# Convolution taps of a two-layer decoder trunk: none beside layer A's output products, more beside layer B's input products

## The chip, the cores and the metric

The kernel runs on one core of a Trainium2 chip, as one program. The metric is the device time of an execution in microseconds. Three runs of the kernel before give a median of 1700.62 us (1698.21 to 1704.68). Five engines work side by side, each through its own queue in order: TensorE (PE, matrix products and transposes), VectorE (DVE), ScalarE (ACT), GpSimd (POOL) and SyncE (SP, which issues transfers).

## What is computed

Two layers on x, 2048 rows of 1024 columns in float32. Each layer l first makes u = x * (1 + scale) + shift, with shift, scale and gate from the vector c. The mixer of layer A is

```
[a | g | z] = u W_in + b_in;  h = a * sigmoid(g)
h = causal depthwise conv_31(h) + b_conv;  h = LayerNorm_channels(h);  h = swish(h)
y = (h * silu(z)) W_out + b_out
```

and that of layer B

```
[B | C | v | z] = u W_in;  y = (B * conv_3(C * v) * silu(z)) W_out
```

and both end in x <- LayerNorm(alpha * x + gate * y). The convolution with 31 taps is per channel, along the rows.

## The kernel before

**Products.** The rows are cut into two halves (sc 0 and 1), and each half into two quarters of 512 rows, so that quarters q = 0 to 3 exist. An input product W_in for a half is done with seven products of half the size in place of eight (a Strassen form, class Pair: the seven parts of a pair of weight blocks). Each of the seven is 12 matmuls of 512 columns (four blocks, each operand split into a high and a low part). A list fixes their order (order_of). TensorE's instructions are kept in the order of the program; the instructions of the other engines are ordered by a planner at build time, which takes the ready instruction that stands earliest in the program, with instructions inside `urgent()` ahead of the rest.

**Stages.** Layer A's input products for half 0, then for half 1 (12 pairs each, tiles pxa, pya, pza and pxz, pyz, pzz); layer A's output products for quarters 0 and 1 (tile po); layer B's input products for half 0 (16 pairs, 112 products; tiles pxc, pyc, pzc, pxb, pyb, pzb); layer A's output products for quarters 2 and 3; layer B's input products for half 1; layer B's output products for the four quarters. The input of layer B is made in the output blocks: evacuate (L842, L843, L846, L848), the power on GpSimd (L849), finish (L809, L812), the transposes of columns (tile ptx) and L834, and then the sums and splits of u_stages (join; L279 and L225 on tiles ub). For layer B's first half the weights are made in the stage (L355, L357 on VectorE, splits L224 on ScalarE and L225 on GpSimd) and stored; for its second half they are loaded as stored.

**The long convolution.** It runs on VectorE, one tap an instruction (L572, mac). For each of the 8 blocks of 128 channels and each half of the rows conv_a puts 47 steps into the queue todo: begin (a load of h on SP's queue, preparations on ScalarE and GpSimd), 27 taps of the even and odd positions into two PSUM banks (pca, pcb), turn, out_even (L604, the first result), both_less (L610), 15 taps of the sum of both (pca, pcd), and out_odd (L625, the second result). A result is a tile of tag acc, of which there are three (BUFS), and the convolution's banks are two (BANKS, conv). given stores a result on SP's queue and defers statistics by LAG = 8 ticks: four transposes on TensorE (tile pl) and four bn_stats on VectorE (L668), after which the result's buffer is free. While a norm is being made, statistics wait (held).

**What sets how many steps are issued.** Behind each product or output group stands a call of tick, which takes as many steps from todo as its rate says, carries the fraction on, and then runs what has been deferred to this tick:

```
        due_taps[0] += taps
        conv_steps(int(due_taps[0]))
        due_taps[0] -= int(due_taps[0])
```

The rates are in RATE: a = 3.2 a product in layer A, b = 3.4 a product in layer B's first half, o = 1 for each of the 16 groups of a quarter's output products (run_out). From the sixth part of the last pair but one on (the place `(a, 6)` in ending) the norm of the quarter runs beside the last 9 products, and there the rate is 1. Ahead of it need(q) issues four steps at a time, with no product between, until the quarter's statistics are all there. A planner's order isn't the order of issue: VectorE may do a step before or after the product behind which it is issued.

The same code runs ending for layer A's second half (q = 0) and for layer B's first half (q = 2), and run_out for quarters 0 and 1 with taps still in todo, and for quarters 2 and 3 with todo empty.

Of the kernel before, what the change touches and what calls it, by code (L numbers as in the profile page):

```python
# [30 lines left out]
BOOST = 100000  # L31
BUFS = dict(u=56, raw=4, s=1, w=5, ta=8, hin=1, xk=2, xs=1, pt=1, acc=3, tv=2, uf=6)
BANKS = dict(mm=4, tp=2, conv=2)
RATE = dict(a=3.2, b=3.4, o=1)
LAG = 8
LEAD = 3

# [2 lines left out]
def hybrid_trunk(ctx, tc, x, c, ada_w, ada_b, a_w_in, a_b_in, a_conv_w, a_conv_b,  # L40
# [42 lines left out]
    def flush(after=None):  # L83
        with ExitStack() as order:
            if after is not None:
                order.enter_context(tc.issue_after(after.ins))
            for dst, src, _ in late:
                nc.scalar.dma_start(dst, src)
        for *_, then in late:
            if then is not None:  # L90
                then()
        late.clear()
# [24 lines left out]
    def tick(taps, *gens):  # L117
        clock[0] += 1
# [3 lines that stand above are left out]
        for gen in gens:  # L122
            next(gen, None)
        due = [job for at, job in waiting if at <= clock[0]]
        waiting[:] = [w for w in waiting if w[0] > clock[0]]
        for job in due:
            job()
# [299 lines left out]
    def product(pair, p, ks=range(KH)):  # L427
        for i in ks:
            pair.mm(p, i)
            if i == KH - 1:  # L430
                pair.evacuate(p)
# [238 lines left out]
    def conv_steps(n):  # L670
        for _ in range(min(n, len(todo))):
            todo.popleft()()
# [106 lines left out]
    def out_rows(q, l):  # L779
        wide = lambda ap: (lambda h: ap[:, h * T:(h + 1) * T].broadcast_to([P, T]))  # L780
        rows = [row_tiles(f"g{l}_{q}", wide(post_ln_g[l:l + 1, :])),
                row_tiles(f"b{l}_{q}", wide(post_ln_b[l:l + 1, :]))]
        if l == 0:
            rows.append(row_tiles(f"gb{q}", lambda h: gb_dram[h]))
        return rows
# [183 lines left out]
    def queue_convs():  # L969

        while wanted and all(wanted[0] + (hf,) in windows for hf in range(2)):
            conv_a(*wanted.popleft())
# [103 lines left out]
    for n, (p, r) in enumerate(order_a):  # L1076
# [9 lines left out]
        queue_convs()  # L1086
        tick(1 if (p, r) in moves else RATE["a"])
    flush()
# [3 lines left out]
    norms = {q: a_norm(q, gs[0, q]) for q in range(NQ)}  # L1092
# [3 lines left out]
    def begin_out(q, l, rows):  # L1096
        if l == 0:
            fu[q] = [st("u", [P, T], f"ub{q}_{k}") for k in range(K)]
        outs[l, q] = mixer_out(q, l, gs[l, q], rows, fu.get(q))
        next(outs[l, q])  # L1100
# [7 lines left out]
    def run_out(l, q, *beside):  # L1108
        for _ in outs[l, q]:
            tick(RATE["o"], *beside)  # L1110
        for gen in beside:
# [12 lines left out]
    def need(q):  # L1124

        while emitted[q] < K:
            tick(4)

    def ending(pairs, order, rate, q, *beside):

        a, b = len(pairs) - 2, len(pairs) - 1
        gens = list(beside)
        for p, r in order:
            if (p, r) == (b, 5):
                rows = out_rows(q, 0)
            if (p, r) == (a, 6):
                need(q)
                gens.append(norms[q])
            product(pairs[p], r)
            queue_convs()  # L1140
            tick(1 if norms[q] in gens else rate, *gens)
        for gen in gens:
            for _ in gen:
                pass
        flush()
        begin_out(q, 0, rows)
        return rows

    rows = ending(pa[1], order_a, RATE["a"], 0, back)
    need(1)  # L1150
    run_out(0, 0, wait(6, norms[1]))
# [12 lines left out]
    def with_join(sc, order):  # L1164
        for n, at in enumerate(order):
            if n == 6:
                join(sc)
            yield at

    for pair in pb[0]:  # L1170
        pair.adds = (nc.vector, nc.gpsimd)
    rows = ending(pb[0], with_join(0, order_b), RATE["b"], 2)
    need(3)
    run_out(0, 2, wait(6, norms[3]))
# [46 lines left out]
```

## Time and profile before

| | |
|---|---|
| median of three runs | 1700.62 us |
| the profiled execution's own time | 1698.88 us |
| its span, first to last instruction | 1696.8 us |
| mean granted clock of TensorE | 0.963 |
| busy: TensorE, VectorE, ScalarE, GpSimd | 92%, 69%, 39%, 57% |

The span is 2.1 us shorter than the execution's own time. The rows further down are of this one execution. A row of the timeline gives the start, the duration, engine, line, operation, output and input, a count, and in brackets the idle time ahead of it and what ended it. In a table by stretch each engine has its busy time and its instructions, and then come TensorE's granted clock (1.00 is full speed), the share of the transfer engines and their rate. Stages by their first matmul: layer A's output products of quarter 0 at 588.5 us, layer B's first input product at 696.9; in the second half the same places are at 1077.3 and 1179.2.

### The profile page before, as it was taken

The numbers are of one execution on the slowest core, as the hardware profiler recorded it, in microseconds if no ns is written. First come the engines' busy times: TensorE is split into PE (matmuls) and PEld (weight loads), VectorE is DVE, ScalarE is ACT, GpSimd is POOL, SyncE is SP. The second block draws the span as 40 slices with busy tenths as digits, with TensorE's granted clock in tenths as the row PEclk, the third lists the DMA queues.
The fourth block names the chain that finished last, engine by engine and source line by source line (L and its number), as shares of the span: only waits on it lengthen the run. The fifth ranks groups of instructions, "written<-read, shape, count | busy, mean of one in ns | idle before, by whom it ended". The sixth has DMA issues, their size and how long they took to land.

```text
span 1696.8 us, 20882 instructions
## 1 busy us (share of the span) xinstructions
PE 1568.5 (92%) x6828; PEld 1267.6 (75%) x6828; DVE 1171.5 (69%) x1820; ACT 665.7 (39%) x1134; POOL 963.8 (57%) x808
## 2 busy tenths in 40 slices
PE   5899998799998998869998998999899999999996
PEld 5777787678887777647777886777688888778884
DVE  6669999978988988888999953574822222225565
ACT  3544445655433436543444334254632221212221
POOL 5788878775654245866888786537655531221110
PEclk9799999899999999979999999999899999999999
DMA  9478888799999997526777767976689886778995
GB/s 271 157 275 294 293 302 302 243 350 363 330 371 352 359 329 242 196 96 240 270 241 254 268 247 270 385 255 236 221 281 301 297 302 215 247 268 267 336 333 209
DMA packets 237916, 469.63 MB, mean 277 GB/s; under 512 B 20329, under 2 KB 102641, under 8 KB 237809
## 3 DMA queue, kind: packets, MB, share of 16 engines
q1 hardware_dynamic: 190864, 323.06, 56.8%
q10 hardware_dynamic: 46944, 145.25, 22.1%
q8 instruction: 54, 0.88, 0.2%
q14 instruction: 54, 0.43, 0.1%
HBM read 297.72 MB, written 170.52 MB: 276 GB/s over the span
## 4 chain that ended last, share of the span: by engine, by line
PE 52%; DVE 21%; DMA 12%; POOL 7%; issue 5%; ACT 2%; ACTq 0%; SPq 0%; DVEq 0%; POOLq 0%
PE po L98 19%; PE pxb L98 6%; PE pxc L98 6%; DVE pca L572 5%; PE pxa L98 4%; DVE pcb L572 4%; PE pzb L98 3%; DMA keptb<-wb 3%; PE pzc L98 3%; DMA keptc<-wc 2%; PE pza L98 2%; PE pxz L98 2%; DMA wr<-w_dram 2%; PE pyc L98 1%; DVE pcd L572 1%
## 5 line engine op out<-in xcount | busy, mean ns | idle before, releaser
L572 DVE SCALAR_TENSOR_TENSOR pcb<-h,w,pcb 128x512 f32<-128x512 f32 x224 | 166.5, 743 | 9.0 <-ACT pcb L580 8.6
L572 DVE SCALAR_TENSOR_TENSOR pca<-h,w,pca 128x512 f32<-128x512 f32 x192 | 142.7, 743 | 0.2
L572 DVE SCALAR_TENSOR_TENSOR pca<-xs,w,pca 128x512 f32<-128x512 f32 x128 | 95.4, 745 | 0.8
L842 DVE TENSOR_TENSOR r<-po,r 128x512 f32<-128x512 f32 x64 | 43.2, 681 | 68.1 <-PE po L98 49.5
L572 DVE SCALAR_TENSOR_TENSOR pcd<-xs,w,pcd 128x512 f32<-128x512 f32 x112 | 83.2, 743 | 0.1
L517 POOL TENSOR_TENSOR ada<-ada,adaw 128x512 f32<-128x512 f32 x48 | 63.6, 1325 | 34.4 <-ACT adaw L511 14.3
L812 ACT ACTIVATE r<-r,nb,rs 128x512 f32<-128x512 f32 x64 | 47.2, 809 | 81.3 <-DVE nb L809 81.2
L225 POOL TENSOR_TENSOR gb_0l<-vb,gb_0h 128x512 fp32r<-128x512 f32 x4 | 5.2, 1292 | 111.2 <-ACT gb_0h L224 111.2
L547 POOL TENSOR_TENSOR wf<-wf,grow 128x512 f32<-128x512 f32 x32 | 42.4, 1331 | 38.2 <-DMA wf<-in_b_w_out_dram 33.4
L849 POOL TENSOR_TENSOR rs<-rs,mhalf 128x1 f32<-128x1 f32 x32 | 18.3, 584 | 75.5 <-DVE rs L848 75.5
L586 POOL TENSOR_TENSOR lead<-lead,part 128x512 f32<-128x512 f32 x32 | 43.6, 1361 | 22.0 <-ACT part L585 22.0
L911 POOL TENSOR_TENSOR hb1c<-c12c,c22c 128x512 f32<-128x512 f32 x16 | 21.1, 1322 | 59.6 <-DVE c22c L403 59.6
L225 POOL TENSOR_TENSOR wc<-rawc,wc 128x512 fp32r<-128x512 f32 x32 | 45.1, 1409 | 16.8 <-ACT wc L224 16.7
L511 ACT ACTIVATE adaw<-adaw,cond 128x512 f32<-128x512 f32 x64 | 42.4, 715 | 30.4 <-DMA adaw<-in_ada_w_dram 27.4
L225 POOL TENSOR_TENSOR wf<-wf 128x512 fp32r<-128x512 f32 x32 | 42.9, 1350 | 17.6 <-ACT wf L224 17.6
L821 DVE TENSOR_TENSOR r<-r,g 128x512 f32<-128x512 f32 x48 | 39.0, 825 | 20.1 <-PE ptx L101 17.7
L803 POOL TENSOR_TENSOR r<-r,gb 128x512 f32<-128x512 f32 x32 | 44.8, 1416 | 13.3 <-DMA r<-in_x_dram 11.5
L834 ACT ACTIVATE ub<-ptx,post_sh,post_sc 128x128 f32<-128x128 f32 x128 | 47.2, 487 | 12.9 <-PE ptx L101 12.9
L225 POOL TENSOR_TENSOR wb<-sb,wb 128x512 fp32r<-128x512 f32 x24 | 35.3, 1473 | 23.7 <-ACT wb L224 23.7
L225 POOL TENSOR_TENSOR wb<-rawb,wb 128x512 fp32r<-128x512 f32 x32 | 44.7, 1398 | 6.3 <-ACT wb L224 4.0
L225 POOL TENSOR_TENSOR wa<-rawa,wa 128x512 fp32r<-128x512 f32 x32 | 44.9, 1407 | 4.0 <-ACT wa L224 2.4
L756 ACT ACTIVATE v<-v,second_columns 128x512 f32<-128x512 f32 x32 | 25.9, 814 | 51.0 <-DVE v L755 50.8
(1388 smaller groups left out, 5582.9 us busy)
## 6 DMA issues: line engine op xcount, KB each, us to landing
wr<-w_dram SPq DMA_DIRECT2D x128, 512.0 KB
kepta<-wa ACTq DMA_DIRECT2D x56, 512.0 KB
wa<-kepta SPq DMA_DIRECT2D x56, 512.0 KB
keptc<-wc ACTq DMA_DIRECT2D x56, 512.0 KB
keptb<-wb ACTq DMA_DIRECT2D x56, 512.0 KB
wc<-keptc SPq DMA_DIRECT2D x56, 512.0 KB
wb<-keptb SPq DMA_DIRECT2D x56, 512.0 KB
adaw<-in_ada_w_dram SPq DMA_DIRECT2D x32, 512.0 KB
```

The costliest lines, as they stand in the source:

```text
L98: return tc.keep_in_program_order(nc.tensor.matmul(*args, **kw))
L225: made = (eng or nc.gpsimd).tensor_tensor(lo, src, hi.bitcast(F32), op=ALU.subtract)
L511: nc.scalar.activation(raw[:, j], raw[:, j], AF.Identity, scale=cond[:, kk + j:kk + j + 1])
L517: nc.gpsimd.tensor_tensor(acc, acc, raw[:, j], op=ALU.add)
L547: nc.gpsimd.tensor_tensor(w[:, 1], w[:, 1], grow, op=ALU.mult)
L572: nc.vector.scalar_tensor_tensor(out=tiles[out], in0=src, scalar=w, in1=tiles[acc], op0=ALU.mult, op1=op)
L586: nc.gpsimd.tensor_tensor(lead, lead, part, op=ALU.add)
L803: nc.gpsimd.tensor_tensor(rt, rt, gb[0][h], op=ALU.add)
L812: nc.scalar.activation(rts[t, h], rts[t, h], AF.Identity, scale=rs, bias=nb)
L821: eng.tensor_tensor(r, r, g[h], op=ALU.mult)
L834: nc.scalar.activation(fs[k][:, t * P:(t + 1) * P], pt[:, j * P:(j + 1) * P], AF.Identity, scale=post_sc[:, k:k + 1], bias=post_sh[:, k:k ...
L842: nc.vector.tensor_tensor(r, pss[t], r, op=ALU.add)
```

## The change

Two rates and the number of steps beside a norm. In ending and run_out no steps are issued beside a norm and beside layer A's output products; behind each of layer B's input products of the first half 3.8 steps are issued instead of 3.4. (RATE's o serves layer B's output products as well, where todo is empty.)

```diff
--- before.py
+++ after.py
@@ -31,7 +31,7 @@
 BOOST = 100000
 BUFS = dict(u=56, raw=4, s=1, w=5, ta=8, hin=1, xk=2, xs=1, pt=1, acc=3, tv=2, uf=6)
 BANKS = dict(mm=4, tp=2, conv=2)
-RATE = dict(a=3.2, b=3.4, o=1)
+RATE = dict(a=3.2, b=3.8, o=0)
 LAG = 8
 LEAD = 3
 
@@ -1138,7 +1138,7 @@
                 gens.append(norms[q])
             product(pairs[p], r)
             queue_convs()
-            tick(1 if norms[q] in gens else rate, *gens)
+            tick(0 if norms[q] in gens else rate, *gens)
         for gen in gens:
             for _ in gen:
                 pass
```

## Rows read from the trace of the kernel before

**Rows 1.** The page: busy times of the engines, shares of the last chain.

```profile
PE 1568.5 (92%) x6828; PEld 1267.6 (75%) x6828; DVE 1171.5 (69%) x1820; ACT 665.7 (39%) x1134; POOL 963.8 (57%) x808
PE 52%; DVE 21%; DMA 12%; POOL 7%; issue 5%; ACT 2%; ACTq 0%; SPq 0%; DVEq 0%; POOLq 0%
```

**Rows 2.** Busy time by stretch: PE, PEld, DVE, ACT, POOL; clock, transfer share, GB/s.

```profile
651.00:697.00 46.00, 41.37 (x187) 32.47 (x185) 39.58 (x60) 20.36 (x48) 34.85 (x28) 0.93 0.79 254
697.00:766.30 69.30, 48.97 (x178) 35.53 (x177) 59.59 (x83) 38.82 (x80) 46.88 (x36) 0.78 0.32 119
777.00:971.60 194.60, 184.01 (x799) 147.63 (x798) 185.67 (x288) 78.20 (x132) 153.61 (x135) 0.98 0.70 249
766.30:1005.60 239.30, 228.62 (x998) 183.81 (x997) 213.84 (x334) 96.33 (x163) 188.56 (x165) 0.99 0.70 252
980.00:1041.00 61.00, 58.56 (x258) 47.23 (x258) 25.53 (x45) 20.05 (x34) 44.15 (x39) 1.00 0.72 255
...
1136.20:1179.20 43.00, 39.19 (x178) 31.07 (x177) 20.87 (x31) 18.68 (x44) 33.29 (x27) 0.96 0.65 214
1179.20:1227.10 47.90, 42.69 (x178) 32.72 (x177) 38.94 (x55) 32.73 (x69) 31.16 (x17) 0.89 0.70 238
```

**Rows 3.** By stretch, the taps (L572) alone: VectorE's busy time, clock, transfers.

```profile
614.30:660.20 45.90, 0.00 (x0) 0.96 0.74 255
660.30:714.00 53.70, 29.42 (x42) 0.87 0.63 202
714.00:777.00 63.00, 0.00 (x0) 0.81 0.44 163
777.00:971.60 194.60, 119.94 (x168) 0.98 0.70 249
```

**Rows 4.** Timeline of VectorE at two second results of convolutions.

```profile
658.91 0.88 DVE L668 BATCH_NORM_STATS2 s<-pl 128x6 f32<-128x128 f32 x4
659.71 0.67 DVE L625 TENSOR_TENSOR acc<-pca,acc 128x512 f32<-128x512 f32 x1
...
773.45 0.88 DVE L668 BATCH_NORM_STATS2 s<-pl 128x6 f32<-128x128 f32 x4
774.25 0.67 DVE L625 TENSOR_TENSOR acc<-pca,acc 128x512 f32<-128x512 f32 x1
```

**Rows 5.** Groups of the page: GpSimd's additions in begin.

```profile
L586 POOL TENSOR_TENSOR lead<-lead,part 128x512 f32<-128x512 f32 x32 | 43.6, 1361 | 22.0 <-ACT part L585 22.0
```

**Rows 6.** Groups by line, 777 to 971.6, VectorE: the convolutions' results.

```profile
L604 DVE SCALAR_TENSOR_TENSOR acc<-pca,second_columns,pt 128x512 f32<-128x512 f32 x4 | 3.0, 745 | 2.1 <-ACT pt L599 2.1
L625 DVE TENSOR_TENSOR acc<-pca,acc 128x512 f32<-128x512 f32 x4 | 2.7, 686 | 0.2
```

**Rows 7.** Timelines at layer B's start, first half, then second half.

```profile
697.03 0.74 DVE L572 SCALAR_TENSOR_TENSOR pcd<-xs,w,pcd 128x512 f32<-128x512 f32 x1
697.68 0.68 DVE L842 TENSOR_TENSOR r<-po,r 128x512 f32<-128x512 f32 x1
...
703.94 1.97 PE L101 MATMUL ptx<-ident,r 128*128 128x128 f32 x8 [4.17 <-ACT r L812]
...
706.13 0.63 PE L98 MATMUL pyc<-ub00b21l,wc 128*128 128x512 f32 x1
706.56 0.63 PE L98 MATMUL pyc<-ub00b21h,wc 128*128 128x512 f32 x1
...
724.35 5.12 DVE L279 TENSOR_TENSOR ub<-ub,ub 128x512 f32<-128x512 f32 x3
...
1183.00 0.39 PE L98 MATMUL pyc<-ub10b21l,wc 128*128 128x512 f32 x1
1183.23 0.40 PE L98 MATMUL pyc<-ub10b21h,wc 128*128 128x512 f32 x1
...
1198.58 3.09 DVE L279 TENSOR_TENSOR ub<-ub,ub 128x512 f32<-128x512 f32 x5
```

**Rows 8.** TensorE's waits on VectorE, 766.3 to 1005.6: total, times, longest.

```profile
PE pxb L98 <- DVE c22b L403: 2.3, 1, 2.3
```

## Prediction

> **What bounds the kernel now.** I read the page's busy shares first: TensorE is busy 92% of the span, VectorE 69%, and in the chain that ended last TensorE has 52% and VectorE 21% [rows 1]. So TensorE sets the time, and VectorE where it makes TensorE wait. The table by stretch shows where that is [rows 2]. Layer A's second output block of the first half (651 to 697) takes 46.0 us, its twin in the second half (1136.2 to 1179.2), which does the same output products with no taps about, 43.0. The start of layer B (697 to 766.3, its first 12 products) takes 69.3 us against 47.9 in the twin; VectorE is busy 59.6 of the 69.3 and TensorE has a mean clock of 0.78. Then, from product 13 to 91 (766.3 to 1005.6), TensorE is busy 228.6 of 239.3 us, while VectorE in the inner part of that, 777 to 971.6, is busy 185.7 of 194.6, or 95%. From 980 to 1041, with the convolutions over, it is busy only 25.5 of 61.
>
> The table of the taps alone holds the key [rows 3]: no tap in 614.3 to 660.2, 42 taps (29.4 us) in 660.3 to 714, none in 714 to 777, then 168 taps in 120 us, four convolutions. The timeline says why [rows 4]: the second result of a convolution (L625) starts right behind the statistics (L668) of an earlier one, at 659.71 behind 658.91, at 774.25 behind 773.45. There are three buffers for these results (tag acc), a result gives its buffer back when its statistics have been taken, and the transposes of the statistics stand in TensorE's fixed order, eight ticks behind the step that makes the result. So VectorE takes taps as early as it is free, well ahead of where the program issues them, until it has no buffer for a result; then the two convolution banks are held too and it takes none.
>
> **The change part by part.** By the loops, a convolution is 47 steps, 16 of them make 752. When the first norm enters, nine products before the end of layer A's input products, 440 are issued in both kernels. Before, those 9 products and twice 16 output groups issue one each, 41 more; after, none. Layer B's products then have 271 steps at 3.4 (done with product 80), after the change 312 at 3.8 (done with product 83). All 312 still come ahead of the second half's norms (product 104), so nothing has to be caught up in a loop without products.
>
> *The steps themselves.* None is added or removed. The 41 hold one load and two stores of a convolution on SP's queue, one set of ScalarE and GpSimd preparations and 39 VectorE instructions. As VectorE already ran these long before their place in the program, their being issued later costs nothing in itself; the cover is that same run ahead, and the preparation of one convolution more inside layer B (two additions of 1.36 us on GpSimd and a third like them, about 4 us) lies beside 188.6 busy of 239.3 [rows 2, 5]. If that cover fails, it is at most those 4 us, inside the range below.
>
> *The statistics move.* Convolutions 10's two results are steps 453 and 470, 11's are 500 and 517. Before, the statistics of 10 come in the output blocks. After, step 453 is issued with layer B's 4th product and its statistics stand behind the 12th, those of 470 behind the 16th. Convolution 11's second result needs the buffer that the 12th product's statistics free. So the 42 taps of convolution 12 that ran in 660 to 714 can't start before about the 12th product: the pause that now lasts from 614 to 660 lasts to about 760. That is a move of one whole convolution, 29.4 us of taps and about 2.2 us of its three results (3 x 0.74) [rows 3, 6].
>
> *What the output block and layer B's start gain.* The bounds are the twins: 46.0 - 43.0 = 3.0 us, and 69.3 - 47.9 = 21.4 us [rows 2]; below, zero, as the planner could order the rest no better. Of the first I take 2: two groups of statistics leave TensorE and VectorE there. Of the second I take 7. TensorE waits 4.17 us for the normalised rows, and the matmuls behind it run at 0.43 us apart instead of 0.23, the lower clock (1.2 GHz) after the idle time, which is 12 x 0.2 = 2.4 us for that product; the twin keeps 0.23 [rows 7]. Between the rows' evacuations VectorE ran taps, and one tap is 0.66 us of delay each time [rows 7]. The rest of the 21.4 I leave: in the twin, the weights are loaded as kept, here they are made, with GpSimd's splits beside VectorE's subtractions, three of which took 5.12 us where five took 3.09 in the twin [rows 7]. That stays. Gain: **9 us**.
>
> *What layer B pays.* From product 13 to 91 VectorE must now do five convolutions, not four. One costs 120 / 4 + 2.2 = 32.2 us; the other work in 777 to 971.6 is 185.7 - 4 x 32.2 = 57 us over some 64 products, 0.9 us each. So 5 x 32.2 + 79 x 0.9 = 232 us, and at the 95% that VectorE reaches now, 243 us, against 239.3 that TensorE takes for these products today [rows 2, 3, 6]. The last statistics now stand behind product 91 instead of 88. That is 4 us too long, and about 1 more for the hand over at the end: **5 us**. The lower bound is 0, since TensorE's 10.7 us of idle time there overlap with it. The upper bound is a coupling: 3.8 steps of 32.2 / 47 = 0.685 us and 0.9 us are 3.50 us a product, at 95% 3.67, against 239.3 / 79 = 3.03 now. At product 13 VectorE has 516 steps done where 489 are issued; it does (3.03 x 0.95 - 0.9) / 0.685 = 2.89 steps a product, loses 0.91, and its lead of 27 is gone 30 products later. If TensorE then had to follow VectorE for the remaining 40, that is 40 x 0.64 = 26 us. I take 5, nearer the lower end, because TensorE waits for VectorE only once in these products today, 2.3 us, with VectorE at 95% already [rows 8].
>
> **The sum.** -9 + 5 = -4 us. The profiled execution takes 1698.9 us, 2.1 around its span, 1.7 under the median of the runs, 1700.6; on the median I forecast 1696.6, no change that can be told (0.5% is 8.5 us, about what a measurement of this kernel can tell from none).
>
> **The rivals.** *Faster.* Layer B's start comes near its twin, and the longer work of VectorE is hidden behind TensorE's present waits: 2 + 14 gained, 1 paid, 1685.6. For it: VectorE is busy nearly through 697 to 760 and all its taps there go; from 980 on it has 35 us of room that three more products reach into. Against: the subtractions and the making of the weights stay.
>
> *Slower.* VectorE becomes the bound of layer B. The place is products 43 to 83, the price 26 us; it decides from where the 27 steps of lead are used up and the older taps are taken before the additions of the weights. With the 9 us gained it gives +17, 1717.6. For it: 95% busy already, and 3.67 us a product against 3.03. Against: the one wait of 2.3 us [rows 8], and that the instructions TensorE waits for stand inside `urgent()`, ahead of the taps; only the additions for weights don't. The Trainium skill bears on this in Perfetto Trace Analysis, section Identifying the Most-Contended Engine: where a kernel has regimes with different busiest engines, it says, interleaving them may help. Here the change does the reverse, from blocks with idle VectorE time to one without; by that rule the sum would be the slower rival's, by the rows alone it is -4. The trace so far bears out the full engine, and not that TensorE is held by it.
>
> *No effect.* The planner still finds room for convolution 12 before layer B, because buffers come free in another way than I read it; then it is 1700.6, in the same band as my forecast.
>
> **How the numbers follow.** Forecast 0.35 and no effect 0.08 make 0.43 for no change over 0.5%. The faster rival 0.32: only 4.5 us lie between the forecast and the bound of 8.5. The slower rival 0.25: gain and price are each known to within their bounds only, and the price has the longer end. The range of 8 in 10 goes from 1681 (the faster rival and 5 us more of the twin's time) to 1720 (the slower one and 2 us); the two ends of all bounds, -24 and +26, are left out. The forecast's own range is 1692 to 1705.
>
> **What the profile after would show.** Right: no tap from about 614 until the statistics behind layer B's 12th product; L625 of convolution 11 directly behind L668 at that place; the stretch of layer B's first 12 products near 60 us with the 4.17 us wait gone; VectorE at 95% or more, and convolution 16's L625 near product 88 instead of 79. Wrong: taps again between 660 and 714 (no effect); the first 12 products at 69 us (no gain); a product of layer B above 3.3 us from the 43rd on with TensorE waiting for weights or evacuations (slower); the start under 55 us and products still at 3.03 (faster).

## The result, and the profile after

The changed kernel takes 1714.54 us (median of five runs, 1713.86 to 1716.54) against 1700.62 for the kernel before (also the median of five runs, 1698.21 to 1704.68): a ratio of 1.0071 with a 95% interval of 1.0046 to 1.0097. That is slower, by 13.9 us between the medians and 12 by the ratio. The forecast, 4 us faster, has the wrong sign; the time lies inside the range.

The page of the kernel after gives the span, the busy shares and the shares of the last chain. They answer to [rows 1].

```profile
span 1712.1 us, 20862 instructions
PE 1564.7 (91%) x6828; PEld 1265.7 (74%) x6828; DVE 1179.8 (69%) x1820; ACT 667.0 (39%) x1134; POOL 965.3 (56%) x808
PE 55%; DVE 18%; DMA 10%; POOL 7%; issue 6%; ACT 3%; SPq 1%; ACTq 0%; DVEq 0%; POOLq 0%
```

The counts are the same as before, and TensorE's and VectorE's busy times have moved by 4 and 8 us. The span is 15.3 us longer, so the difference is time in which TensorE waits. The chain doesn't say where: VectorE's share of it even falls, from 21% to 18%. The table by stretch does: layer A's output products of quarter 1, layer B's first 12 products, its products 13 to 91, and those up to layer A's second pair of output blocks. Columns as in [rows 2].

```profile
651.60:698.10 46.50, 40.07 (x177) 31.84 (x176) 19.71 (x27) 16.86 (x42) 33.90 (x27) 0.93 0.73 231
698.10:764.70 66.60, 46.78 (x180) 34.05 (x179) 53.02 (x64) 38.32 (x80) 43.43 (x31) 0.82 0.33 124
764.70:1020.50 255.80, 231.70 (x1004) 185.82 (x1002) 242.23 (x378) 101.79 (x171) 192.51 (x170) 0.97 0.68 244
1020.50:1089.70 69.20, 61.70 (x263) 48.33 (x261) 38.27 (x56) 29.46 (x47) 47.52 (x41) 0.97 0.82 296
```

VectorE is busy only 19.7 us of the output block where it was 39.6 [rows 2], and the block is no shorter, 46.5 us for 46.0. The first 12 products take 66.6 us instead of 69.3. Products 13 to 91 take 255.8 us instead of 239.3: 16.5 us more, a little over the 15.3 by which the spans differ. The stretch behind them (69.2 us) gives 2.7 back, the output blocks of quarters 2 and 3 take 106.1 us for 101.9.

Where the taps went is as forecast. The taps (L572) alone, to be held against [rows 3]:

```profile
614.40:766.60 152.20, 0.00 (x0) 0.89 0.55 191
766.60:1019.30 252.70, 148.91 (x210) 0.97 0.68 244
```

No tap runs for 152 us, and then five convolutions' 210 taps (168 before) run inside layer B. VectorE's timeline shows what ends the pause and where the work ends, as [rows 4] did:

```profile
765.19 0.88 DVE L668 BATCH_NORM_STATS2 s<-pl 128x6 f32<-128x128 f32 x4
765.99 0.67 DVE L625 TENSOR_TENSOR acc<-pca,acc 128x512 f32<-128x512 f32 x1
...
972.47 0.69 DVE L625 TENSOR_TENSOR acc<-pca,acc 128x512 f32<-128x512 f32 x1
...
1019.31 0.68 DVE L625 TENSOR_TENSOR acc<-pca,acc 128x512 f32<-128x512 f32 x1
```

Convolution 11's second result follows directly on the statistics behind product 12, as predicted; the result at 972.47 is the last but one convolution's, about when the last came before (971.57), and the last now comes at 1019.31.

What TensorE waits for in products 13 to 91 (total, times, longest):

```profile
PE pl L101 <- DVE acc L604: 6.1, 2, 4.2
PE pl L101 <- DVE acc L625: 6.0, 2, 4.6
PE pzc L98 <- ACT wc L224: 5.4, 2, 4.9
PE pzc L98 <- POOL wc L225: 2.5, 4, 0.8
```

The first two rows, 12.1 us, are new; before, TensorE waited for VectorE there once [rows 8]. They are not waits of products. They are the transposes of statistics (tile pl), which stand in TensorE's fixed order eight ticks behind the step that makes the result. VectorE has fallen so far behind that TensorE gets there first: behind products 74, 78, 86 and 91. TensorE's timeline at the second of them:

```profile
968.25 0.39 PE L98 MATMUL pyb<-ub03b21h,wb 128*128 128x512 f32 x1
973.22 1.12 PE L101 MATMUL pl<-ident,acc 128*128 128x128 f32 x4 [4.59 <-DVE acc L625]
973.99 0.78 PE L98 MATMUL pzb<-ub00t1h,wb 128*128 128x512 f32 x1
974.56 0.63 PE L98 MATMUL pzb<-ub00t1l,wb 128*128 128x512 f32 x1
974.99 0.63 PE L98 MATMUL pzb<-ub00t1h,wb 128*128 128x512 f32 x1
```

The 4.59 us wait ends 0.75 us after L625 started at 972.47. A product that needs nothing of the result stands behind it. The matmuls then start 0.43 us apart, where those ahead of the wait stood at 0.23. The granted clock is 0.50 from 974 to 976, the lower level (1.2 GHz), and was 1.00 from 960 to 968, so the wait costs more than itself.

### The profile page after: what moved, and what is told of

Its sections match the earlier page's. It is cut to its first block, busy times and chain, and to the rows that moved or that the text cites. A ratio compares the mean times of both kernels' runs of the same rounds, so it can differ in the third digit from the quotient of the medians.

```text
span 1712.1 us, 20862 instructions
## 1 busy us (share of the span) xinstructions
PE 1564.7 (91%) x6828; PEld 1265.7 (74%) x6828; DVE 1179.8 (69%) x1820; ACT 667.0 (39%) x1134; POOL 965.3 (56%) x808
## 4 chain that ended last, share of the span: by engine, by line
PE 55%; DVE 18%; DMA 10%; POOL 7%; issue 6%; ACT 3%; SPq 1%; ACTq 0%; DVEq 0%; POOLq 0%
PE po L98 16%; PE pxc L98 6%; PE pxb L98 6%; PE pxa L98 6%; DVE pca L572 4%; PE pzb L98 3%; PE pzc L98 3%; PE pza L98 3%; DVE pcb L572 3%; PE pxz L98 2%; PE pyb L98 2%; PE pya L98 1%; PE pyc L98 1%; PE pzz L98 1%; POOL wc L225 1%
## 5 line engine op out<-in xcount | busy, mean ns | idle before, releaser
L572 DVE SCALAR_TENSOR_TENSOR pcb<-h,w,pcb 128x512 f32<-128x512 f32 x224 | 166.6, 744 | 8.8 <-ACT pcb L580 8.4
L572 DVE SCALAR_TENSOR_TENSOR pca<-h,w,pca 128x512 f32<-128x512 f32 x192 | 142.7, 743 | 0.1
L572 DVE SCALAR_TENSOR_TENSOR pca<-xs,w,pca 128x512 f32<-128x512 f32 x128 | 95.4, 745 | 0.9
L572 DVE SCALAR_TENSOR_TENSOR pcd<-xs,w,pcd 128x512 f32<-128x512 f32 x112 | 83.3, 744 | 0.1
L225 POOL TENSOR_TENSOR gb_0l<-vb,gb_0h 128x512 fp32r<-128x512 f32 x4 | 5.2, 1294 | 109.1 <-ACT gb_0h L224 109.1
L225 POOL TENSOR_TENSOR wf<-wf 128x512 fp32r<-128x512 f32 x32 | 43.0, 1355 | 19.6 <-ACT wf L224 14.4
L803 POOL TENSOR_TENSOR r<-r,gb 128x512 f32<-128x512 f32 x32 | 43.4, 1375 | 17.1 <-DMA r<-in_x_dram 13.3
L225 POOL TENSOR_TENSOR wc<-rawc,wc 128x512 fp32r<-128x512 f32 x32 | 47.0, 1468 | 6.8 <-ACT wc L224 6.2
L225 POOL TENSOR_TENSOR wb<-rawb,wb 128x512 fp32r<-128x512 f32 x32 | 45.0, 1406 | 9.5 <-ACT wb L224 9.3
L225 POOL TENSOR_TENSOR wb<-sb,wb 128x512 fp32r<-128x512 f32 x24 | 34.8, 1450 | 27.2 <-ACT wb L224 24.6
L225 POOL TENSOR_TENSOR wa<-rawa,wa 128x512 fp32r<-128x512 f32 x32 | 44.4, 1390 | 5.9 <-ACT wa L224 5.9
```

The lines of the kernel that those rows point to most:

```text
L225: made = (eng or nc.gpsimd).tensor_tensor(lo, src, hi.bitcast(F32), op=ALU.subtract)
L572: nc.vector.scalar_tensor_tensor(out=tiles[out], in0=src, scalar=w, in1=tiles[acc], op0=ALU.mult, op1=op)
L803: nc.gpsimd.tensor_tensor(rt, rt, gb[0][h], op=ALU.add)
```

## The experiments

The theory after the result: **due dates**. Five convolutions fit into layer B only if their results are due late enough; with the late start (no steps beside the output products) and the early due date (3.8 steps a product) together, VectorE falls behind, and TensorE waits at pl. The rivals: a busier VectorE slows the products as such (**pace**); the waits come from the small number of result buffers (**window**); or the loss has nothing to do with the taps. "Kernel before" and "after" below name the kernel that is edited, and each ratio is to the kernel before on the same chip. Spans of stages in the texts below are from first matmul to first matmul. Stages are read from one profiled execution of each kernel, and executions of one kernel lie 3 to 19 us apart. The profile of the first experiment (e1_after_b34) is the shortest of its kernel's twelve executions, 10.7 us under their median, that of e5_after_b42 is 5.9 us above its median and that of e10_b34_vec2 4.5; the others lie within 2.1 us of theirs. Two stages that differ by a few us don't show that the kernels differ.

### One part of the change at a time

The kernel after, with the due date put back:

```diff
-RATE = dict(a=3.2, b=3.8, o=0)
+RATE = dict(a=3.2, b=3.4, o=0)
```

> The changed kernel with layer B's rate back at 3.4 (no steps beside norms and output products stays). Due-date theory: TensorE lost its time at the statistics of the last convolutions, which wait for results that VectorE finishes too late. At 3.4 the 312 steps are issued by product 92 and the last statistics stand behind product 100 instead of 91, some 25 us later, so VectorE is in time: waits of the statistics on L604 and L625 go from 12 us to under 2, and the time from +14 to within 4 us of the kernel before. Rival, total load: VectorE has a convolution more to do in layer B whatever the rate, and TensorE follows it: still +10 or more. Rival, chance order: the planner's new order is the cause, +8 to +16 whatever the rate.

Measured: 1703.34 us, ratio 1.0019 (0.9999 to 1.0040). First 12 products and products 13 to 91:

```profile
695.00:762.00 67.00, 46.82 (x182) 34.24 (x180) 54.59 (x64) 38.52 (x80) 44.25 (x31) 0.80 0.33 123
762.00:1000.30 238.30, 228.40 (x995) 182.78 (x993) 228.79 (x354) 99.48 (x169) 190.48 (x168) 0.99 0.72 256
```

The pause of the taps is as long as in the kernel after (none from 614 to 763), and VectorE is busy 96% of products 13 to 91, more than the 94.7% of the kernel after. Yet they take 238.3 us, and no wait at pl is left. The work that doesn't fit runs after product 91: the last result comes at 1010.3, ten us into the next stretch, and is due some nine products later. So a full VectorE needn't slow the products. As this profile is the shortest execution of its kernel, the reading has to stand in another run too; it does in the third experiment below.

The kernel before, with the early due date alone, and with the late start beside the output products alone:

```diff
-RATE = dict(a=3.2, b=3.4, o=1)
+RATE = dict(a=3.2, b=3.8, o=1)
```

> The kernel before with layer B's rate at 3.8 alone (one step beside each norm product and output group stays). Due-date theory: convolution 12 still runs ahead in the output block (42 taps between 660 and 714), VectorE ends its convolutions at about 972 as before, and the last statistics move from behind product 88 to behind product 80, that is to about 974: waits of 0 to 5 us at the last two statistics, time +0 to +5 us. Rival, pace: 3.8 steps a product crowd VectorE in every product and that alone is the loss: +10 to +16 us.

Measured: 1697.85 us, ratio 0.9997 (0.9976 to 1.0018). The 42 taps run between 659 and 714 as in the kernel before, the last result comes at 971.65 and the transpose that needs it runs at 973.80 without a wait.

```diff
-RATE = dict(a=3.2, b=3.4, o=1)
+RATE = dict(a=3.2, b=3.4, o=0)
```

> The kernel before with no steps beside output groups alone (RATE o 0; one step beside each norm product and 3.4 stay). Due-date theory: step 453 is issued with layer B's 2nd product, its statistics stand behind the 10th, so the pause of the taps reaches into layer B as in the changed kernel (none from 614 to about 755); the last statistics stand behind product 98, so no waits on results: within 4 us of the kernel before. Rival, total load: +10 or more, as the convolution moved is the same.

Measured: 1699.63 us, ratio 1.0010 (0.9991 to 1.0029), no tap from 614 to 754 and no wait at pl. Its profile lies 0.2 us from the kernel's median. Products 13 to 91:

```profile
761.50:1001.20 239.70, 227.81 (x994) 181.46 (x993) 230.53 (x355) 98.75 (x168) 188.22 (x167) 0.99 0.73 256
```

VectorE is again busy 96% of them, and they take no longer than in the kernel before. The pace rival falls.

The last result shows how much room each kernel has: the transposes that need it start 25 us after it starts in the kernel before (at 996.4 us, and the result at 971.6), 15 us after it in the first experiment, 2 in the second, 20 in the third, and in the kernel after TensorE waits for it. Neither the late start alone (the first run, and this one in part) nor the early due date alone costs anything that can be told; only both together cost 0.7%.

### More of the cause, and less work for the due date

The kernel after with 4.2 steps a product:

```diff
-RATE = dict(a=3.2, b=3.8, o=0)
+RATE = dict(a=3.2, b=4.2, o=0)
```

> The changed kernel with layer B's rate at 4.2. Due-date theory, with its size from the trace of the changed kernel: from the 12th product on VectorE has five convolutions to do, 161 us, and 1.07 us of other work a product; at 4.2 the last statistics stand behind product 83 instead of 91, so up to there VectorE needs (161 + 71 x 1.07) / 0.95 = 250 us where TensorE needs 71 x 3.03 = 215. Waits on results at the statistics rise from 12 us to about 30, and the time to +26 to +36 us over the kernel before. Rival, chance order: another order, anywhere from +5 to +16.

Measured: 1727.36 us, ratio 1.0172 (1.0148 to 1.0195). TensorE's waits in products 13 to 91, which take 269.0 us:

```profile
PE pl L101 <- DVE acc L625: 18.7, 3, 7.5
PE pl L101 <- DVE acc L604: 7.1, 3, 3.5
```

They grow from 12.1 to 25.8 us, the stretch from 255.8 to 269.0 (this profile is the longest of four executions). The other way round, the kernel after with 35 taps of its last convolutions left out, so that the same results are due at the same place with less work:

```diff
-                todo.append(lambda r=r: tap_s(R // 2 + r))
+                todo.append((lambda: None) if sc and e > 2 else
+                            (lambda r=r: tap_s(R // 2 + r)))
```

> The changed kernel without the seven taps into pcd of each of convolutions 12 to 16 (35 taps left out, so those output columns are another sum; the steps are still counted). Window theory: VectorE has 35 x 0.7 = 24 us less to do between the 12th and the 91st product, 234 instead of 258, under TensorE's 239: waits on results at the statistics under 2 us and the time within 5 us of the kernel before. Rival, chance order: +8 or more remains.

Measured: 1697.27 us, ratio 1.0000 (0.9982 to 1.0018). The waits at pl are gone, and products 13 to 91 take:

```profile
759.00:1002.90 243.90, 230.34 (x1001) 183.56 (x1000) 217.43 (x341) 100.09 (x170) 192.14 (x169) 0.99 0.71 252
```

217.4 us of VectorE work where the kernel after had 242.2: 24.8 less work gives back 11.9 us of the stretch, and the ratio falls from 1.0071 to 1.0000. Late results are the cause from both sides: more of them cost more, and with none the loss is gone.

### Due later, or more buffers

The kernel after, with the statistics of convolutions 10 to 16 four ticks later in TensorE's order and everything else kept:

```diff
-            defer(LAG, lambda: statistics(e, q, y))
+            defer(LAG + (4 if sc and e else 0), lambda: statistics(e, q, y))
```

> The changed kernel with the statistics of convolutions 10 to 16 twelve ticks behind the result instead of eight. Window theory: the last due date moves from product 91 to 95, but the buffer that lets convolution 12 begin comes free with the 16th product instead of the 12th; the window stays 79 products and so does the loss: +10 to +18 us over the kernel before, VectorE without taps until about 775. Due date alone: four products (12 us) more room for VectorE, the waits all but vanish: +5 us or less.

Measured: 1703.20 us, ratio 1.0020 (1.0006 to 1.0035). Products 13 to 91 take 246.7 us. The waits at pl are down to 7.4 us, of which the 5.0 lie in that stretch and the 2.4 behind product 95:

```profile
PE pl L101 <- DVE acc L604: 5.0, 1, 5.0
PE pl L101 <- DVE acc L625: 2.4, 1, 2.4
```

This falls between the two expectations: the time is where the due dates put it, the waits haven't vanished. A later place for the statistics alone takes the ratio from 1.0071 to 1.0020, as the due dates would have it; some of the waits stay, as the window would have it, since a result that is transposed later also keeps its buffer longer (convolution 11's L625 moves from 766.0 to 774.7). The run doesn't part the two cleanly.

So the kernel after, and then the kernel before, with a fourth result buffer. To make room, one buffer of tag tv goes and its tile part moves to tag pt:

```diff
-BUFS = dict(u=56, raw=4, s=1, w=5, ta=8, hin=1, xk=2, xs=1, pt=1, acc=3, tv=2, uf=6)
+BUFS = dict(u=56, raw=4, s=1, w=5, ta=8, hin=1, xk=2, xs=1, pt=1, acc=4, tv=1, uf=6)
...
-                part = st("tv", [P, T], f"part{name}_{r}")
+                part = st("pt", [P, 1 + T], f"part{name}_{r}")[:, :T]
```

> The changed kernel with four buffers for results instead of three (room for it by giving ScalarE's part of the preparations the buffer of tag pt, so that tv is 1). Buffer theory: convolution 11's second result has a buffer at once, so convolution 12 runs in the output block as in the kernel before, up to its own first result's need; taps between 614 and 700 are 40 or so instead of 0, the waits on results at the statistics fall from 12 us to under 4, and the time to within 5 us of the kernel before. Rival, issue order: taps that are issued late are run late whatever the buffers; taps there stay at 0 and the time at +12 to +16.

Measured: 1710.13 us, ratio 1.0063 (1.0037 to 1.0090): the waits at pl are gone, and the loss isn't. Products 13 to 91:

```profile
766.90:1015.60 248.70, 232.63 (x1003) 187.69 (x1001) 217.24 (x341) 97.37 (x165) 189.77 (x168) 0.97 0.69 245
```

They still take 9.4 us more than in the kernel before, with VectorE busy only 87% of them; TensorE's waits for the weights' parts (L224, L225) are 14.1 us there (8.2 before). Late results aren't the reason in this kernel. (This alone doesn't speak for the window against the due dates, since with a fourth buffer the start isn't late either.) The expectation of the time was missed, and so was that of the place of the taps (22 of the expected 40 ran from 614 to 700). Layer A's first output block grew too. Its taps, in this kernel and then in the kernel after:

```profile
585.30:655.20 69.90, 22.62 (x32) 0.95 0.81 295
```

```profile
589.60:651.60 62.00, 9.02 (x12) 0.97 0.85 310
```

A fourth buffer lets VectorE run further ahead, here into the block where TensorE waits for VectorE's evacuations: 69.9 us instead of 62.0.

> The kernel before with four buffers for results (and the preparations' part in the buffer of tag pt). Theory from the fourth run: taps that fill VectorE beside a quarter's output products delay the evacuations there, whatever is issued when: 25 or more taps instead of 13 between the first output product and the first transposes of rows, that stretch grows from 62.6 to 67 to 71 us, no waits on results in layer B, and the time is +4 to +12 us. Rival: the earlier convolution is free there and gives VectorE room in layer B: within 3 us, or faster.

Measured on the kernel before: 1709.84 us, ratio 1.0073 (1.0049 to 1.0097), 32 taps (22.67 us) in that block, which takes 67.7 us where the kernel before takes 62.6 with 13. TensorE's waits there:

```profile
PE po L98 <- DVE r L842: 6.2, 6, 2.1
PE po L98 <- ACT c21z L707: 1.8, 1, 1.8
```

Before, these were 3.6 us (once) and 0.7. So the three buffers also keep VectorE out of a block where more of its taps go with a longer stage. The block is 5 of the 13 us by which the two profiles differ; products 13 to 91 take 244.3 us, 5 more as well, with 8.3 us of waits for ScalarE's parts of the weights (L224 on wc, 3.2 before). How much of the 12 us (by the ratio) comes from the one buffer fewer of tag tv stays open, as the two edits weren't parted.

### Why layer B's start gained so little

What TensorE waits for in the first 12 products of the kernel after:

```profile
PE pzc L98 <- DVE ub00t1l L225: 6.6, 1, 6.6
PE ptx L101 <- ACT ub L834: 4.3, 4, 2.1
PE pzb L98 <- DVE c12c L403: 3.8, 1, 3.8
```

With no tap about, TensorE still waits 6.6 us for a sum's low part, as before (6.8). VectorE is slow there for another reason: its subtractions L279 and L225 share the time with GpSimd's splits of the weights. Two experiments take GpSimd's splits away. First the kernel after, with ScalarE copying both parts of the first three pairs' weights:

```diff
-                split(src, wt[:, 0], wt[:, 1])
+                if self.plain:
+                    nc.scalar.copy(wt[:, 0], src)
+                    nc.scalar.copy(wt[:, 1], src)
+                else:
+                    split(src, wt[:, 0], wt[:, 1])
...
+    for pair in pb[0][:3]:
+        pair.plain = True
```

> The changed kernel in which the first three pairs of layer B's weights get both parts as copies on ScalarE, without GpSimd's subtraction (their low parts hold the full weight, so the result is another one). Theory on the missing gain: layer B's first 12 products stay at 66.6 us although no tap runs there, because GpSimd's splits and VectorE's subtractions hold each other up: the stretch falls by 6 to 14 us, to between 52 and 61, and VectorE's L279 and L225 there fall towards 0.7 us each. Rival: the stretch is bound by the chain of sums and splits itself or by the making of the weights on VectorE and ScalarE: it stays within 3 us of 66.6.

Measured: 1694.32 us, ratio 0.9973 (0.9947 to 0.9999); the first 12 products:

```profile
696.30:754.90 58.60, 44.29 (x182) 32.57 (x180) 46.79 (x64) 43.84 (x92) 22.00 (x19) 0.91 0.39 141
```

58.6 us instead of 66.6, with GpSimd busy 22.0 us instead of 43.4. The waits at pl are 7.9 us still. Then a version that does the whole computation: the kernel of the first experiment (3.4 steps, none beside the output products), with the low parts of the first two pairs' weights on VectorE:

```diff
-                split(src, wt[:, 0], wt[:, 1])
+                split(src, wt[:, 0], wt[:, 1], self.low)
...
+    for pair in pb[0][:2]:
+        pair.low = nc.vector
```

> The first run's kernel (no steps beside norms and output products, 3.4 in layer B), with the low parts of the weights of layer B's first two pairs subtracted on VectorE instead of GpSimd (the result is the reference's). Theory on the missing gain: the two engines' instructions on the same stretch hold each other up, so 14 subtractions at 0.7 us on VectorE cost less than the stretching they end: the first 12 products fall from 67 to 59 to 64 us and the time to 3 to 8 us under the kernel before. Rival: VectorE is the bound of that stretch anyway: it stays at 67 or grows to 72, and the time is at or above the kernel before.

Measured: 1693.81 us, ratio 0.9970 (0.9953 to 0.9987). The first 12 products and products 13 to 91:

```profile
697.60:754.50 56.90, 44.59 (x181) 33.51 (x180) 49.93 (x74) 37.93 (x80) 25.65 (x21) 0.85 0.40 144
754.50:1001.00 246.50, 230.25 (x995) 182.72 (x994) 232.02 (x357) 99.12 (x169) 184.08 (x165) 0.99 0.71 247
```

In the first 12 products VectorE has ten instructions more than in the first experiment and 4.7 us less to do: the mean of the twelve sums L279 on tile ub falls from 989 ns in the kernel after to 719 (768 in the run with ScalarE's copies). Products 13 to 91 take eight us more than in the first experiment's profile, but that one lies far under its kernel's median and this one above, so it isn't shown that they give the gain back. By the ratios the kernel is 0.5%, or 8 us, faster than the first experiment's (0.9970 against 1.0019, the intervals apart), most of the ten us of layer B's start. It is 0.3% under the kernel before and about 1% under the kernel after (1.0071), and the lowest ratio of a kernel that does the whole computation, though not told apart from the next one.

The same edit in the kernel before, and for the first pair only in the first experiment's kernel:

> The kernel before, all rates as they were, with the low parts of the weights of layer B's first two pairs on VectorE. Theory: the gain of the tenth run is that of layer B's start, and taps beside it cost little: the first 12 products fall from 69.4 to 58 to 64 us here too, and the time to 2 to 6 us under the kernel before. Rival: it needs a VectorE free of taps there, as in the tenth run: the stretch stays above 66 and the time within 2 us of the kernel before, or above.

Measured: 1694.32 us, ratio 0.9983 (0.9964 to 1.0002). The first 12 products take 64.1 us, just outside what was expected at its upper end, 5.2 under the kernel before, and the output block ahead of them 51.1 instead of 46.0: with the 42 taps about, what is gained in the one is lost in the other. The profile is shorter than that of the kernel before in products 13 to 91 (235.9 us for 239.3), which the expectation didn't have, and the interval of the ratio holds 1. So it isn't shown that the kernel before gains by this edit.

> The tenth run's kernel with only the first pair's low parts on VectorE. Theory: it is the first pair's weights that are made beside the sums and splits of layer B's input; one pair gives half or more of the gain: the first 12 products take 58 to 63 us, the time is 2 to 8 us under the kernel before. Rival: the second pair's (743 to 755 us) matter as much: above 63 us and within 2 us of the kernel before.

Measured: 1699.84 us, ratio 0.9998 (0.9980 to 1.0015). The first 12 products take 57.1 us, a little less than expected, so the first pair is all that counts there. The expected time was missed: of the 12 us that the start gains on the kernel before, the median shows nothing. In its profile the stretch behind product 91 takes 78.0 us, where the kernel before has 71.9; why isn't known.

## Why the prediction was wrong

**The move of the taps: right.** The three result buffers, not the place of issue, set when taps run; the pause reaches to the statistics behind product 12, and five convolutions lie inside layer B. Each of these signs appeared where it was named, but for the end of the last convolution: product 91, not 88.

**The gain of 9 us: about 2.** The output block's 2 us didn't come (46.5 us for 46.0). Of the 7 us at layer B's start 2.7 came. The 4.17 us wait of [rows 7] is gone, and pyc's matmuls start 0.23 us apart, as the step said. But the time went to the next waits of the same chain, for the sums and splits beside GpSimd's weights: 6.6 us as before, and 3.8 for c12c where it was 1.1. The second experiment keeps all 42 taps and its start takes 67.4 us; the first and the third have none and take 67.0 and 67.8. So the taps weren't what bound that start as long as GpSimd's splits lie beside it. The step did say that GpSimd's splits "stay"; what it missed is that with them the rest of the gain stays out: without them the start takes 56.9 to 58.6 us with no tap about, and 64.1 with the taps.

**The price of 5 us: 16.5.** This is the step that failed (*What layer B pays*), and its mis-sized term is "0.9 us each" for VectorE's other work beside a product; 1.02 is measured. It was read in the inner stretch, 777 to 971.6, and applied to all 79 products. The outer row of the same group [rows 2] was there to be read: 213.84 - 4 x 32.2 - 0.7 (one more second result, at 774.25) is 84.3 us over 79 products, 1.07 each, as the products at both ends have more such work. Then 5 x 32.2 + 0.7 + 84.3 is 246 us, at 95% 259, against 243 in the prediction. Measured are 242.2 us of VectorE work in 255.8; less 5 x 32.2 and 0.7 that is 80.5, or 1.02 a product. With the due date behind product 91, 259 against 239.3 is a price of some 20 us instead of 4: the term alone is worth the sign. With a later due date the same work costs nothing that can be told, as the first and the third experiment show.

**Where the price appears.** The prediction looked for waits at weights and evacuations. It did say that "the last statistics now stand behind product 91", and put that at 4 us of a full VectorE; but the waits are at these very statistics, 12.1 us at pl, with the half clock behind them. The lead of 27 that "is gone 30 products later" was the reckoning that comes nearest, and it sat in the upper bound instead of the sum. It left out the eight ticks by which the statistics stand behind their step: 8 x 3.8 = 30 steps more of room. At the prediction's own rates (27 + 30) / 0.91 is 63 products, so TensorE would wait from about product 76 on, not 43, and 15 products at 0.64 us make about 10 us. The first wait stands behind product 74, and the four make 12.1 us. The reason given for the lower end, one wait of 2.3 us with VectorE at 95%, said nothing of this: before the change the last result was there 25 us ahead of its transposes.

**The slower rival: right sign and close time, wrong place.** It gave 1717.6 us, within 3.1 us of the measured time by luck: 9 us gained where about 2 were, and 26 paid where 16.5 were. Its mechanism, older taps ahead of the additions of the weights, isn't what decides: TensorE's waits on weights in products 13 to 91 are 10.9 us, in the kernel before 8.2. The sentence of the Trainium skill cited with it (Perfetto Trace Analysis; it stands in the section Optimization Strategy, behind the one that the prediction names), that interleaving regimes may help, would have had the sign. The runs don't bear it out as the reason: the first and the third experiment keep the taps out of the output blocks nearly as far and lose nothing that can be told, and the runs with a fourth result buffer put more taps beside the output products and lose 0.6 to 0.7%.

**Open.** The output blocks of quarters 2 and 3 take 101.9 us before and 106.1 after, but also 100.8 to 107.0 over the other runs, with no order by the edits; what varies there isn't known (the planner's order is one candidate). And the window isn't parted from the due dates: no run gives the results more buffers and leaves all else as it is.

## What to carry to other kernels

Here the moved work cost nothing that could be told until its consumer reached its fixed place ahead of it: ask of each result where its consumer stands in the in-order engine's queue, and compare the arrival of the maker with that of the consumer over the whole stretch, ends included. Moving a start later and a due date earlier can each be free and together cost 0.7%. And where VectorE looks too busy, see first whether its instructions are longer than the same ones elsewhere; here one pair's splits moved off GpSimd shortened a stage by ten us, which no shift of the taps did. Whether the kernel gains by as much is another question: with two pairs it did by 0.3%, with one by nothing that could be told.

## What the runs showed of the hardware

VectorE's subtractions of two operands are longer where GpSimd's splits lie beside them. In the kernel after, VectorE's timeline at layer B's start:

```profile
724.53 4.02 DVE L279 TENSOR_TENSOR ub<-ub,ub 128x512 f32<-128x512 f32 x3
728.48 1.75 DVE L225 TENSOR_TENSOR ub00t1l<-ub,ub00t1h 128x512 fp32r<-128x512 f32 x1
730.15 0.68 DVE L279 TENSOR_TENSOR ub<-ub,ub 128x512 f32<-128x512 f32 x1
```

and the same place with ScalarE's copies in place of GpSimd's subtractions:

```profile
723.19 4.76 DVE L279 TENSOR_TENSOR ub<-ub,ub 128x512 f32<-128x512 f32 x6
727.87 0.68 DVE L225 TENSOR_TENSOR ub00t1l<-ub,ub00t1h 128x512 fp32r<-128x512 f32 x1
```

The same L225 takes 1.75 us and 0.68. One instruction alone shows little, as the stretched ones change from run to run (in the kernel before this one takes 0.68 and four others of L225 about 1.75); the mean of the twelve sums above, 989 against 768 and 719 ns, shows it over the stage. The Trainium skill, SBUF — State Buffer, section Who interferes with whom, states that a VectorE instruction with two inputs in SBUF contends with a GpSimd instruction that reads SBUF; it calls the ports that the two share an exclusive lock. The runs agree in that the stretching goes where GpSimd's splits go; which of the two blocked the other in a given pair isn't shown here.

The other finding is the price of a short wait in the clock: behind the 4.59 us wait above, matmuls stand 0.43 us apart where they stood at 0.23, at a granted clock of 0.50 (1.2 GHz). In 1000 to 1020, where the third wait at pl ends (4.24 us, at 1002.19) and the fourth begins, the mean granted clock is 0.83, and in the same 20 us of the first experiment 1.00.
